# A decoder layer on one core: the second half of an up-projection weight tile is split one work unit later, and the constants are loaded behind the input

## The chip, the cores and the metric

The program runs on one core of a Trainium2 chip. The metric is the device time of one execution in microseconds (us). The runs shown of the kernel before took 1481.33, 1481.35 and 1481.86 us, a median of 1481.35 us.

## The reference, cut to what matters

One layer, 256 tokens, width 2048, everything float32:

```python
def reference(x, p, g_mix, w_in, ..., g_mlp, w_up, w_down, g_ple, w_ple_gate, w_ple_proj):
    h = rmsnorm(x, g_mix)
    proj = h @ w_in                                   # 2048 -> 10240: q, k, v of two mixers, two gates
    qa, ka, va, qb, kb, vb, ga, gb = jnp.split(proj, splits, axis=-1)
    qa = partial_rope(rmsnorm(qa, qn_gain), pos)      # gain and rotation: the constants
    ka = partial_rope(rmsnorm(ka, kn_gain), pos)
    ya = dilated_mixture(qa, ka, va)
    yb = stick_breaking(qb, kb, vb)
    merged = sigmoid(ga) * (ya @ w_branch_a) + sigmoid(gb) * (yb @ w_branch_b)
    x = x + merged @ w_out
    hm = rmsnorm(x, g_mlp)
    x = x + square(relu(hm @ w_up)) @ w_down          # 2048 -> 8192 -> 2048
    hp = rmsnorm(x, g_ple)
    return x + (p @ w_ple_proj) * sigmoid(hp @ w_ple_gate)
```

## The kernel before, in words

Each weight is read from HBM once, in tiles of 1 MB (128 partitions x 8 KB). SP issues these loads (`load`, line 91) into a pool of three buffers called `raw`. A product of two float32 matrices is made of products of their parts: `split` (lines 82 and 83) makes a rounded part `wh` on ACT and the remainder `wl` on DVE, and TensorE (PE) multiplies parts. `split_weights` does this in chunks of 1024 columns; a 1 MB tile gives two chunks. The parts lie in pools of three buffers, `wh` and `wl`. So the next chunk but two can be split only when PE has finished a chunk, and a `raw` buffer is free for the next load when its second chunk has been split.

**The start.** The input stays transposed in `x` (two tiles of 8 rows of 128 features each), the first weights follow in between (`first_weights`, four steps `c`, lines 185 to 204): SP loads a piece of `x`, then the weights that go with it. ACT and DVE make the parts `h` of `x` times gain (lines 85 and 86). The constants (`idt`, an identity for transposes; `cs`, masks and the rotation table; `gq`, the two gains of the norm of q and k) are loaded by POOL's queue at lines 201 to 203. The same queue loads the rows of `x` (`xr`, two tiles of 1 MB, line 229), which lie in the buffers of the two `x` tiles: the first `xr` waits until `x`'s first tile has been read for the last time, the second for the other tile. ACT squares the rows (line 232), and from the sums comes the factor `rt` that scales all results of the first projection; `first_norm` uses it 5 us of the planner's clock behind the first group.

**The MLP.** In stage `s` three streams of work units run interleaved by a table of due times (`together`): the up projection of the next hidden block (`up_units`, 16 units, two per weight tile), a half of the down projection by a fast scheme with seven products (`fast_units`, 7 units, line 545 to 549) and the other half plainly (`plain_units`, 8 units, lines 613 to 615). A generator yields after each unit. An up tile has 16 steps of two matmuls (lines 525 and 526) and yields behind step 7. Results leave PSUM through `add_rows` (line 454, DVE, into `xr`) and through `hidden` (lines 501 to 510). In a fast product, `right` is the sum of a loaded quarter and of `b11`, a further `raw` tile (line 566, DVE).

What stands in which order on an engine is settled when the program is built, by a scheduler that goes by the order of the Python code (its units) and a model of its own. At run time each engine works through its list in order and waits at semaphores.

The lines that the change touches are those of the start and of `up_units`:

```python
            load_rows()
            nc.gpsimd.dma_start(idt, cst[:, C_ID:C_ID + P])
            nc.gpsimd.dma_start(cs, cst)
            nc.gpsimd.dma_start(gq, ...)
...
                parts = split_weights(load(wup[4 * s + g, j], DT, P), DT, P)
                for kt, (wh, wl) in enumerate(parts):
                    ...
                    if kt == 7:
                        yield
```

Of the kernel before, what the change touches and what calls it, by code (L numbers as in the profile page):

```python
# [16 lines left out]
P = 128  # L17
T = 256
D = 2048
DT = D // P  # L20
# [39 lines left out]
def layer_kernel(ctx: ExitStack, tc: tile.TileContext, xt, xm, pt, gains, qkg, cst,  # L60
                 wa, wba, wbb, wo, wup, wdn, wpg, wpp, out):
    nc = tc.nc
# [9 lines left out]
    def block(shape, dtype, name, pool=None):  # L72
        pool = pool or mblk
        return pool.tile(shape, dtype, tag="blk", name=name)

    def bank(tag):
        return psum.tile([P, 512], F32, tag=tag, name=f"ps_{tag}")

    def split(hi, lo, src, scale=None):

        if scale is None:
            nc.scalar.activation(hi, src, AF.Copy)  # L82
            nc.vector.tensor_tensor(lo, src, hi.bitcast(F32), op=ALU.subtract)  # L83
        else:
            nc.scalar.activation(hi, src, AF.Copy, scale=scale)
            nc.vector.scalar_tensor_tensor(lo, src, scale, hi.bitcast(F32),
                                           op0=ALU.mult, op1=ALU.subtract)

    def load(src, nk, cols):
        raw = wts.tile([P, nk, cols], F32, tag="raw", name="raw")  # L90
        nc.sync.dma_start(raw.rearrange("p k c -> p (k c)"), src)
        return raw

    def split_weights(raw, nk, cols, step=None):

        step = step or 1024 // cols
        parts = []
        for k0 in range(0, nk, step):
            n = min(step, nk - k0)
            wh = wts.tile([P, n, cols], F32R, tag="wh", name="wh")  # L100
            wl = wts.tile([P, n, cols], F32R, tag="wl", name="wl")
            split(wh, wl, raw[:, k0:k0 + n, :])
            parts += [(wh[:, i, :], wl[:, i, :]) for i in range(n)]
        return parts
# [11 lines left out]
    def advance(us):  # L116
        clock[0] += us
        while True:
            due = [e for e in pending if e[0] <= clock[0]]
            if not due:  # L120
                return
            e = min(due, key=lambda e: e[:2])
            pending.remove(e)
            e[2](*e[3])

    def flat(a):
        return a.rearrange("p a t -> p (a t)")

    def group_m(chunks, lhs, load=lambda src: weights(src, 4, 512)):

        ps = [bank("mm") for _ in range(2)]
        last, kt = len(lhs) - 1, 0
        for src in chunks:
            for wh, wl in load(src):
                for tt in range(2):
                    t = slice(tt * P, (tt + 1) * P)
                    nc.tensor.matmul(ps[tt], lhs[kt][:, 0, t], wh, start=kt == 0, stop=False)  # L137
                    nc.tensor.matmul(ps[tt], lhs[kt][:, 0, t], wl, start=False, stop=False)  # L138
                    nc.tensor.matmul(ps[tt], lhs[kt][:, 1, t], wh, start=False, stop=kt == last)  # L139
                kt += 1  # L140
                advance(1.3)
        return ps
# [20 lines left out]
    cs = work.tile([P, C_END], F32, tag="cs", name="cs", bufs=1)  # L163
    idt = const.tile([P, P], F32, name="idt")
    gq = const.tile([P, 2, DH], F32, name="gq")
# [6 lines left out]
    def xs(k):  # L172
        return x[k // 8][:, k % 8, :]

    def new_acts(name, n=DT, pool=None):
        tiles = [block([P, 4, 2, T], F32R, f"{name}{i}", pool) for i in range(n // 4)]
        return [tiles[k // 4][:, k % 4, :, :] for k in range(n)]
# [4 lines left out]
    def load_x(a, b):  # L182
        nc.sync.dma_start(x[a // 8][:, a % 8:(b - 1) % 8 + 1, :], xt[:, a:b, :])

    def first_weights(c):

        k = 4 * c
        if c == 0:
            raw = wts.tile([P, 4, 512], F32, tag="raw", name="raw")
            for a, b in ((0, 1), (1, 2), (2, 4)):  # L190
                load_x(a, b)
                nc.sync.dma_start(raw[:, a:b, :].rearrange("p k c -> p (k c)"),
                                  wa[0, 0, :, a * 512:b * 512])
        else:
            load_x(k, k + 4)
            raw = load(wa[0, c], 4, 512)
        for i in range(k, k + 4):
            split(h[i][:, 0, :], h[i][:, 1, :], xs(i), gn[:, 0, i:i + 1])
        if c == 3:
            load_rows()  # L200
            nc.gpsimd.dma_start(idt, cst[:, C_ID:C_ID + P])
            nc.gpsimd.dma_start(cs, cst)
            nc.gpsimd.dma_start(gq, bass.AP(tensor=qkg.tensor, offset=qkg.offset,
                                          ap=[[0, P], [DH, 2], [1, DH]]))
        return split_weights(raw, 4, 512, 1 if c == 0 else 2)
# [19 lines left out]
    def load_rows():  # L225

        xr.extend(block([P, D], F32, f"xr{tt}", blk) for tt in range(2))
        for tt in range(2):
            nc.gpsimd.dma_start(xr[tt], xm[tt])
# [55 lines left out]
    for n, (dst, gain) in enumerate(((qT, gq[:, 0, :]), (kT, gq[:, 1, :]))):  # L285
        for g in range(2):
            if n + g == 0:
                later(5, first_norm, group_m(range(4), h, first_weights))
                continue
            ps = group_m([wa[2 * n + g, c] for c in range(4)], h)  # L290
            for tt in range(2):
                qk_norm(ps[tt], tt, g, gain, dst)
# [89 lines left out]
    for n, dst in enumerate((qS, kS)):  # L382
        for g in range(2):
            later(2, dilated_head, 4 * n + 2 * g)
            later(13, dilated_head, 4 * n + 2 * g + 1)
            ps = group_m([wa[6 + 2 * n + g, c] for c in range(4)], h)
            for tt in range(2):
                raw = work.tile([P, 4, DH], F32, tag="w2", name="sraw", bufs=W2)
# [15 lines left out]
    def cols(g):  # L404
        return slice(g * PIECE, (g + 1) * PIECE)

    for g in range(4):
        later(2, sb_head, 2 * g)
        later(13, sb_head, 2 * g + 1)
        ps = group_m([wa[12 + g, c] for c in range(4)], h)  # L410
        for tt in range(2):
            nc.scalar.activation(ga[tt][:, cols(g)], ps[tt], AF.Copy, scale=rt[:, tt:tt + 1])
    for g in range(4):
        ps = group_m([wba[g, c] for c in range(2)], ya)
        for tt in range(2):
            a = ga[tt][:, cols(g)]
# [17 lines left out]
    for g in range(4):  # L434
        pg = group_m([wa[16 + g, c] for c in range(4)], h)
        sg = []
        for tt in range(2):
            s = work.tile([P, PIECE], F32, tag="w2", name="sg", bufs=W2)
            nc.scalar.activation(s, pg[tt], AF.Sigmoid, scale=rt[:, tt:tt + 1])
            sg.append(s)  # L440
        ps = group_m([wbb[g, c] for c in range(2)], yb)
# [28 lines left out]
    h2 = new_acts("h2_", pool=blk)  # L470
    ss1 = const.tile([P, 2, 4], F32, name="ss1")
    for g in range(4):
        ps = group_m([wo[g, c] for c in range(4)], m)
# [22 lines left out]
    def hidden(s, fast):  # L496

        n = 8 if fast else 4  # L500
        nc.scalar.activation(s, s, AF.Relu)
        r = mw.tile([P, n, P], F32, tag="hr", name="hr", bufs=1)
        nc.scalar.activation(r[:, 0:4, :].rearrange("p a t -> p (a t)"),
                             s.rearrange("p a t -> p (a t)"), AF.Square)
        if fast:
            a21, a11, a22, a12 = (r[:, i, :] for i in range(4))
            nc.vector.tensor_tensor(r[:, 4, :], a11, a21, op=ALU.subtract)
            nc.vector.tensor_tensor(r[:, 5, :], a21, a22, op=ALU.subtract)
            nc.vector.tensor_tensor(r[:, 6, :], r[:, 5, :], a11, op=ALU.subtract)
            nc.vector.tensor_tensor(r[:, 7, :], r[:, 6, :], a12, op=ALU.add)  # L510
        u = hid.tile([P, 2, n, P], F32R, tag="hid", name="u")
        split(u[:, 0], u[:, 1], r)
        return u
# [3 lines left out]
    def up_units(s, out):  # L517

        for g in range(4):
            sums = mw.tile([P, 2, T], F32, tag="hs", name="hs", bufs=2)  # L520
            for j in range(2):
                ps = bank("mm")
                parts = split_weights(load(wup[4 * s + g, j], DT, P), DT, P)
                for kt, (wh, wl) in enumerate(parts):
                    nc.tensor.matmul(ps, wh, flat(h2[kt]), start=kt == 0, stop=False)  # L525
                    nc.tensor.matmul(ps[:, :T], wl, h2[kt][:, 0, :], start=False, stop=kt == DT - 1)  # L526
                    advance(0.347)
                    if kt == 7:
                        yield
                t = mw.tile([P, T], F32, tag="ev", name="ev", bufs=2)  # L530
                nc.scalar.activation(t, ps[:, T:], AF.Copy)
                nc.vector.tensor_tensor(sums[:, j, :], ps[:, :T], t, op=ALU.add)  # L532
                if j == 1:
                    out.append(hidden(sums, (s, 0) in FAST or (s, 1) in FAST))
                yield
# [147 lines left out]
    for _ in up_units(0, hids[0]):  # L683
        pass
# [22 lines left out]
    for g in range(4):  # L707
        ps = [bank("mm") if g % 2 else bank("at") for _ in range(2)]
        for c in range(4):
            for i, (wh, wl) in enumerate(weights(wpg[g, c], 4, PIECE)):  # L710
                kt = 4 * c + i
# [72 lines left out]
```

## Time and profile before

| What | Value |
|---|---|
| Median of the runs | 1481.35 us |
| The profiled execution's own time | 1482.18 us |
| Its span, first to last instruction | 1480.4 us |
| PE (matmul) busy | 1465.0 us, 99% of the span |
| DVE busy | 960.1 us, 65% |
| ACT busy | 822.6 us, 56% |
| POOL busy | 85.5 us, 6% |
| Granted TensorE clock over the span | 0.998 |
| Read from HBM | 297.85 MB, 203 GB/s over the span |

The profiled execution is 0.83 us above the median, and 1.78 us of its time lie outside the span. A matmul counts as busy to its modelled end, and matmuls overlap in the engine, so that a busy PE is not PE at its full rate: where PE loses time is read from the distance of its starts and from its waits.

### The profile page before, as it was taken

What the parts mean: (1) busy time and instruction counts of PE and PEld (TensorE: products, weight loads), DVE (VectorE), ACT (ScalarE), POOL (GpSimd) and SP (SyncE); (2) the same over time, 40 slices, a digit from 0 to 9 for tenths busy, and PEclk for the clock granted to TensorE, in tenths of its full rate; (3) what the DMA queues carried; (4) which work ended last, traced back from release to release, by engine and by line L of the source; (5) the groups of instructions that cost most, each with busy time, mean ns of one, the idle gap of its engine ahead of it and who ended that gap; (6) DMA issues with size and microseconds to landing.
All of it is one profiled execution on the core that took longest, in us unless ns stands there. A gap on an engine that the chain in (4) does not pass through costs nothing.

```text
span 1480.4 us, 17861 instructions
## 1 busy us (share of the span) xinstructions
PE 1465.0 (99%) x6960; PEld 1207.7 (82%) x6960; DVE 960.1 (65%) x1188; ACT 822.6 (56%) x1056; POOL 85.5 (6%) x107
## 2 busy tenths in 40 slices
PE   8999999999999999999999999999999999999998
PEld 6788888888888888888788888888888888888886
DVE  5975555456555555556677768768777777766654
ACT  6544555488834444546655555555555555556553
POOL 0541000000000000000000000000000000000000
PEclk9999999999999999999999999999999999999999
DMA  8555544544455555558677777768777776754562
GB/s 335 193 191 184 171 171 160 181 171 171 170 189 188 193 183 187 199 174 308 200 228 220 234 228 220 235 202 243 224 216 242 217 220 188 232 171 165 206 216 108
DMA packets 46388, 301.10 MB, mean 203 GB/s; under 512 B 5296, under 2 KB 5552, under 8 KB 13152
## 3 DMA queue, kind: packets, MB, share of 16 engines
q1 hardware_dynamic: 39600, 275.01, 53.2%
q0 software_dynamic: 6560, 24.94, 9.1%
q8 instruction: 54, 0.88, 0.2%
q14 instruction: 30, 0.25, 0.0%
q10 hardware_dynamic: 144, 0.02, 0.0%
HBM read 297.85 MB, written 2.10 MB: 203 GB/s over the span
## 4 chain that ended last, share of the span: by engine, by line
PE 94%; DVE 3%; DMA 1%; ACT 1%; issue 1%; SPq 0%; DVEq 0%; ACTq 0%
PE ps_mm L525 16%; PE ps_mm L139 13%; PE ps_mm L138 13%; PE ps_mm L137 13%; PE ps_mm L526 8%; PE ps_mm L615 4%; PE ps_mm L614 4%; PE ps_mm L613 4%; PE ps_at L547 3%; PE ps_at L545 3%; PE ps_at L549 3%; DVE wl L83 1%; PE ps_at L714 1%; PE ps_at L716 1%; PE ps_mm L716 1%; PE ps_mm L714 1%
## 5 line engine op out<-in xcount | busy, mean ns | idle before, releaser
L83 DVE TENSOR_TENSOR wl<-raw,wh 128x1024 fp32r<-128x1024 f32 (+1 forms) x490 | 598.8, 1229 | 396.2 <-ACT wh L82 390.7
L82 ACT ACTIVATE wh<-raw 128x1024 fp32r<-128x1024 f32 (+1 forms) x490 | 515.1, 1054 | 474.5 <-PE ps_mm L139 209.2
L525 PE MATMUL ps_mm<-h,wh 128*128 128x512 f32 x1024 | 365.1, 396 | 0.7 <-ACT wh L82 0.7
L526 PE MATMUL ps_mm<-h,wl 128*128 128x256 f32 x1024 | 287.5, 281 | 2.5 <-DVE wl L83 2.4
L137 PE MATMUL ps_mm<-wh,h 128*128 128x512 f32 x640 | 254.7, 399 | 2.7 <-ACT wh L82 2.7
L138 PE MATMUL ps_mm<-wl,h 128*128 128x512 f32 x640 | 250.4, 391 | 1.8 <-DVE wl L83 1.8
L139 PE MATMUL ps_mm<-wh,h 128*128 128x512 f32 x640 | 250.5, 391 | 0.0
L525 PEld LDWEIGHTS ps_mm<-h,wh 128*128 128x128 f32 x1024 | 192.2, 188 | 45.2 <-ACT wh L82 1.6
L526 PEld LDWEIGHTS ps_mm<-h,wl 128*128 128x128 f32 x1024 | 193.1, 189 | 12.1 <-DVE wl L83 6.9
L137 PEld LDWEIGHTS ps_mm<-wh,h 128*128 128x128 f32 x640 | 120.4, 188 | 28.8 <-ACT wh L82 5.2
L138 PEld LDWEIGHTS ps_mm<-wl,h 128*128 128x128 f32 x640 | 120.7, 189 | 28.3 <-DVE wl L83 4.5
L139 PEld LDWEIGHTS ps_mm<-wh,h 128*128 128x128 f32 x640 | 120.4, 188 | 25.4
L561 POOL DMA_DIRECT2D chain<-in_wdn x42 | 36.3, 864 | 1142.6 <-DVE hs L532 593.8
L615 PE MATMUL ps_mm<-wh,u 128*128 128x512 f32 x256 | 100.2, 391 | 0.0
L614 PE MATMUL ps_mm<-wl,u 128*128 128x512 f32 x256 | 100.2, 391 | 0.0
L613 PE MATMUL ps_mm<-wh,u 128*128 128x512 f32 x256 | 99.9, 391 | 0.0
L83 DVE TENSOR_TENSOR wl<-chain,wh 128x1024 fp32r<-128x1024 f32 x56 | 68.4, 1224 | 29.1 <-ACT wh L82 28.4
L82 ACT ACTIVATE wh<-chain 128x1024 fp32r<-128x1024 f32 x56 | 59.3, 1059 | 48.3 <-PE ps_mm L525 22.6
L547 PE MATMUL ps_at<-wl,u 128*128 128x512 f32 x196 | 80.8, 412 | 0.2 <-DVE wl L83 0.2
L545 PE MATMUL ps_at<-wh,u 128*128 128x512 f32 x196 | 78.9, 402 | 0.0
L549 PE MATMUL ps_at<-wh,u 128*128 128x512 f32 x196 | 77.0, 393 | 0.0
L613 PEld LDWEIGHTS ps_mm<-wh,u 128*128 128x128 f32 x256 | 48.1, 188 | 10.2 <-DVE hs L532 0.3
(198 smaller groups left out, 1737.5 us busy)
## 6 DMA issues: line engine op xcount, KB each, us to landing
raw<-in_wa SPq DMA_DIRECT2D x79, 1024.0 KB, 4.8
raw<-in_wup SPq DMA_DIRECT2D x64, 1024.0 KB, 4.9
raw<-in_wdn SPq DMA_DIRECT2D x50, 1024.0 KB, 4.8
chain<-in_wdn POOLq DMA_DIRECT2D x42, 512.0 KB, 5.8
raw<-in_wo SPq DMA_DIRECT2D x16, 1024.0 KB, 4.8
raw<-in_wpg SPq DMA_DIRECT2D x16, 1024.0 KB, 4.8
raw<-in_wba SPq DMA_DIRECT2D x8, 1024.0 KB, 4.8
raw<-in_wbb SPq DMA_DIRECT2D x8, 1024.0 KB, 4.7
```

The source lines that it names most:

```text
L82: nc.scalar.activation(hi, src, AF.Copy)
L83: nc.vector.tensor_tensor(lo, src, hi.bitcast(F32), op=ALU.subtract)
L137: nc.tensor.matmul(ps[tt], lhs[kt][:, 0, t], wh, start=kt == 0, stop=False)
L138: nc.tensor.matmul(ps[tt], lhs[kt][:, 0, t], wl, start=False, stop=False)
L139: nc.tensor.matmul(ps[tt], lhs[kt][:, 1, t], wh, start=False, stop=kt == last)
L525: nc.tensor.matmul(ps, wh, flat(h2[kt]), start=kt == 0, stop=False)
L526: nc.tensor.matmul(ps[:, :T], wl, h2[kt][:, 0, :], start=False, stop=kt == DT - 1)
L545: nc.tensor.matmul(ps, f[k][:, 0, a, :], wh, start=start and k == 0, stop=False, skip_group_check=not start)
L547: nc.tensor.matmul(ps, f[k][:, 0, a, :], wl, start=False, stop=False, skip_group_check=not start)
L613: nc.tensor.matmul(ps[tt], u[k][:, 0, a, :], wh, start=i + k == 0, stop=False)
L614: nc.tensor.matmul(ps[tt], u[k][:, 0, a, :], wl, start=False, stop=False)
L615: nc.tensor.matmul(ps[tt], u[k][:, 1, a, :], wh, start=False, stop=last)
```

## The change

In step 3 of the start, POOL copies one column of `x`'s second tile into each of the three constants' tiles before it loads them. A load may not overtake the copy, and the copy needs the last piece of `x`: so the three loads start only when `x` has landed. In `up_units` the parts of a tile's second chunk (steps 8 to 15) are made by code behind the `yield`, that is in the second unit of the tile, and not with those of the first chunk.

```diff
@@ first_weights
         if c == 3:
+            for late in (idt, cs, gq.rearrange("p a d -> p (a d)")):
+                nc.gpsimd.tensor_copy(late[:, 0:1], xs(k)[:, 0:1])
             load_rows()
             nc.gpsimd.dma_start(idt, cst[:, C_ID:C_ID + P])
             nc.gpsimd.dma_start(cs, cst)
@@ up_units
-                parts = split_weights(load(wup[4 * s + g, j], DT, P), DT, P)
-                for kt, (wh, wl) in enumerate(parts):
-                    nc.tensor.matmul(ps, wh, flat(h2[kt]), start=kt == 0, stop=False)
-                    nc.tensor.matmul(ps[:, :T], wl, h2[kt][:, 0, :], start=False, stop=kt == DT - 1)
-                    advance(0.347)
-                    if kt == 7:
+                raw = load(wup[4 * s + g, j], DT, P)
+                for k0 in (0, 8):
+                    for i, (wh, wl) in enumerate(split_weights(raw[:, k0:k0 + 8, :], 8, P)):
+                        kt = k0 + i
+                        nc.tensor.matmul(ps, wh, flat(h2[kt]), start=kt == 0, stop=False)
+                        nc.tensor.matmul(ps[:, :T], wl, h2[kt][:, 0, :], start=False,
+                                         stop=kt == DT - 1)
+                        advance(0.347)
+                    if k0 == 0:
                         yield
```

Behind these lines, line numbers grow by 2, and behind `up_units` by 5.

The first place is POOL's list at the start. Before:

```order
L201 DMA idt_84<-in_cst 128x128
L202 DMA cs_83<-in_cst 128x1216
L203 DMA gq_85<-in_qkg 128x256
L229 DMA xr0_247<-in_xm 128x2048
L229 DMA xr1_248<-in_xm 128x2048
```

and now:

```order
L201 COPY idt_84<-x1_74 128x1
L201 COPY cs_83<-x1_74 128x1
L201 COPY gq_85<-x1_74 128x1
L203 DMA idt_84<-in_cst 128x128
L231 DMA xr0_250<-in_xm 128x2048
L231 DMA xr1_251<-in_xm 128x2048
L204 DMA cs_83<-in_cst 128x1216
L205 DMA gq_85<-in_qkg 128x256
```

The loads of `cs` and `gq` moved behind both loads of the rows; the copies and the small load of `idt` stand ahead of the first. On ACT, the two conversions of constants (`tri_r`, `ones_r`) moved from between the first weight splits to behind the first result's scaling (`qraw`).

The second place is DVE in stage 1 of the MLP, around the end of a plain product (`xr0` and `xr1` from `ps_mm`) and of an up tile (`hs`). `raw_6566` and `raw_6569` are the `b11` tile of a fast product in the two kernels, `raw_6592` and `raw_6595` the next up tile. Before:

```order
L566 TENSOR_TENSOR right_6454<-right_6454,raw_6566 128x2048
L532 TENSOR_TENSOR hs_6403<-ps_mm_6404,ev_6473 128x256
L83 TENSOR_TENSOR wl_6502<-raw_6499,wh_6501 128x1024
L83 TENSOR_TENSOR wl_6506<-raw_6499,wh_6505 128x1024
L83 TENSOR_TENSOR wl_6569<-raw_6566,wh_6568 128x1024
L454 SCALAR_TENSOR_TENSOR xr0_247<-ps_mm_6287,r2_5039,xr0_247 128x512
L83 TENSOR_TENSOR wl_6580<-raw_6566,wh_6579 128x1024
L532 TENSOR_TENSOR hs_6403<-ps_mm_6498,ev_6541 128x256
L454 SCALAR_TENSOR_TENSOR xr1_248<-ps_mm_6288,r2_5039,xr1_248 128x512
L83 TENSOR_TENSOR wl_6595<-raw_6592,wh_6594 128x1024
L83 TENSOR_TENSOR wl_6599<-raw_6592,wh_6598 128x1024
```

and now:

```order
L83 TENSOR_TENSOR wl_6505<-raw_6502,wh_6504 128x1024
L537 TENSOR_TENSOR hs_6406<-ps_mm_6407,ev_6476 128x256
L571 TENSOR_TENSOR right_6453<-right_6453,raw_6569 128x2048
L83 TENSOR_TENSOR wl_6525<-raw_6502,wh_6524 128x1024
L83 TENSOR_TENSOR wl_6572<-raw_6569,wh_6571 128x1024
L83 TENSOR_TENSOR wl_6583<-raw_6569,wh_6582 128x1024
L537 TENSOR_TENSOR hs_6406<-ps_mm_6501,ev_6544 128x256
L456 SCALAR_TENSOR_TENSOR xr0_250<-ps_mm_6290,r2_5042,xr0_250 128x512
L456 SCALAR_TENSOR_TENSOR xr1_251<-ps_mm_6291,r2_5042,xr1_251 128x512
L83 TENSOR_TENSOR wl_6598<-raw_6595,wh_6597 128x1024
L456 SCALAR_TENSOR_TENSOR xr1_251<-ps_at_6430,r2_5042,xr1_251 128x512
```

The second split of `b11` moved ahead of `hs` and of both sums, the sum into `right` moved one split further back (between the two splits of one up tile), and the second split of the next up tile moved away from behind its first.

The third place is ACT where stage 1 begins: the splits of an up tile (`raw`) and of the fast product's `chain`. Before:

```order
L82 ACTIVATE wh_6216<-raw_6214 128x1024
L82 ACTIVATE wh_6220<-raw_6214 128x1024
L531 ACTIVATE ev_6187<-ps_mm_6143 128x256
L82 ACTIVATE wh_6245<-chain_6242 128x1024
L501 ACTIVATE hs_6051<-hs_6051 128x512
L503 ACTIVATE hr_6191<-hs_6051 128x512
L82 ACTIVATE wh_6255<-chain_6242 128x1024
```

and now:

```order
L82 ACTIVATE wh_6219<-raw_6217 128x1024
L82 ACTIVATE wh_6244<-chain_6241 128x1024
L536 ACTIVATE ev_6190<-ps_mm_6146 128x256
L82 ACTIVATE wh_6254<-chain_6241 128x1024
L503 ACTIVATE hs_6054<-hs_6054 128x512
L505 ACTIVATE hr_6194<-hs_6054 128x512
L82 ACTIVATE wh_6266<-raw_6217 128x1024
```

The chunks are now split in the order of the units: first half of the up tile, the two of the fast product, second half of the up tile.

## Rows read from the trace of the kernel before

**Rows 1.** The page's head, and where PE waited (line waited for: us, times, longest).

```profile
span 1480.4 us, 17861 instructions
...
PE ps_mm L526 <- DVE wl L83: 2.4, 5, 0.5
...
PE ps_mm L525 <- ACT wh L82: 0.7, 1, 0.7
PE ps_at L547 <- DVE wl L83: 0.2, 1, 0.2
```

**Rows 2.** The chain that ended last, in order of time (start us, us, what).

```profile
24.13 9.70 DMA xr<-in_xm
```

**Rows 3.** Timeline of ACT, then PE, where the second row tile lands.

```profile
33.86 0.63 ACT L232 ACTIVATE junk<-xr 128x512 f32<-128x512 f32 x1 [3.49 <-DMA xr<-in_xm]
...
34.49 1.04 ACT L82 ACTIVATE wh<-raw 128x1024 fp32r<-128x1024 f32 x1
...
36.84 0.50 PE L138 MATMUL ps_mm<-wl,h 128*128 128x512 f32 x1 [0.41 <-DVE wl L83]
```

**Rows 4.** Table by stretch: us, each engine's busy time, clock, DMA share, GB/s.

```profile
4.00:8.00 4.00, 2.84 (x8) 1.05 (x6) 1.05 (x2) 0.79 (x2) 0.00 (x0) 1.00 0.93 289
...
24.00:34.00 10.00, 10.00 (x45) 8.26 (x44) 3.58 (x3) 5.57 (x12) 0.53 (x1) 1.00 0.96 395
```

**Rows 5.** DMA of 4 to 8 us: POOL's queue (q0), packets, MB, share.

```profile
q0 software_dynamic: 186, 0.73, 58.9%
```

**Rows 6.** DMA issues up to 40 us: KB each, median us to landing.

```profile
cs<-in_cst POOLq DMA_DIRECT2D x1, 608.0 KB, 6.3
```

**Rows 7.** Timeline of SP and POOL at the start; then landing times of x's pieces.

```profile
7.83 0.33 SPq L183 DMA_DIRECT2D x<-in_xt  x1
...
1.27 0.71 POOL L201 DMA_DIRECT2D idt<-in_cst  x1 [0.82 <-POOLq L775]
...
14.88 0.53 POOL L229 DMA_DIRECT2D xr<-in_xm  x1 [11.81 <-DMA x<-in_xt]
...
DMA to landing us min/median/max: 2.4/8.0/12.7
```

**Rows 8.** Timeline of DVE, then PE, in stage 1 of the MLP.

```profile
842.65 1.23 DVE L83 TENSOR_TENSOR wl<-raw,wh 128x1024 fp32r<-128x1024 f32 x1
843.80 0.42 DVE L532 TENSOR_TENSOR hs<-ps_mm,ev 128x256 f32<-128x256 f32 x1
844.13 0.74 DVE L454 SCALAR_TENSOR_TENSOR xr<-ps_mm,r,xr 128x512 f32<-128x512 f32 x1
844.79 2.35 DVE L83 TENSOR_TENSOR wl<-raw,wh 128x1024 fp32r<-128x1024 f32 x2
...
844.96 0.39 PE L549 MATMUL ps_at<-wh,u 128*128 128x512 f32 x1
845.19 0.39 PE L525 MATMUL ps_mm<-h,wh 128*128 128x512 f32 x1
846.06 0.39 PE L526 MATMUL ps_mm<-h,wl 128*128 128x256 f32 x1 [0.48 <-DVE wl L83]
```

**Rows 9.** Timeline of ACT just before that.

```profile
841.56 1.06 ACT L82 ACTIVATE wh<-raw 128x1024 fp32r<-128x1024 f32 x1 [1.73 <-PE ps_mm L525]
```

**Rows 10.** Timeline of SP and DVE around the sum into right; then the page's DMA issues.

```profile
825.02 0.33 SPq L91 DMA_DIRECT2D raw<-in_wdn  x1
...
831.93 2.28 DVE L566 TENSOR_TENSOR right<-right,raw 128x2048 f32<-128x2048 f32 x1
...
raw<-in_wdn SPq DMA_DIRECT2D x50, 1024.0 KB, 4.8
```

**Rows 11.** Timeline of DVE in the first norms; then POOL's smallest products by tile.

```profile
41.96 0.69 DVE L251 TENSOR_TENSOR qsq<-qraw 128x512 f32<-128x512 f32 x1
...
47.37 1.78 DVE L251 TENSOR_TENSOR qsq<-qraw 128x512 f32<-128x512 f32 x1
...
L265 POOL TENSOR_TENSOR ro<-qn,cs x32: 311/322/1339, 48.7 to 118.0; 128x64 f32<-128x64 f32 x32
```

## The prediction

> **What bounds the kernel now.** I read the page's head and its list of PE's waits first. PE is busy for 99% of the span, and its waits in the MLP are few: 2.4 us in five waits of L526 for a `wl`, 0.7 us in one of L525 for a `wh`, 0.2 us in one of L547 for a `wl` [rows 1]. So PE bounds nearly everything, and a change of order can give back only what PE loses in such places, and what it loses at the start. In both orders as written out, the mixers between roughly 60 and 670 us are the same.
>
> For the start I read the chain of waits, then the timelines. One transfer stands on the chain there: the second tile of rows, `xr`, 9.70 us from 24.13 [rows 2]. ACT idles 3.49 us for it, squares its rows at 33.86, and only then makes the next weights' `wh` at 34.49; PE, which wants the remainder of these weights, starts late, at 36.84, with 0.41 us of waiting [rows 3]. So PE's stream is tied here to the landing at 33.83 (24.13 + 9.70): whatever earlier work gains is kept only as far as this landing comes earlier too.
>
> What makes it late is the bandwidth: between 24 and 34 us the DMA engines are busy for 0.96 of the time and move 395 GB/s, between 4 and 8 us for 0.93 but at 289 GB/s [rows 4]. In the latter stretch the constants' queue takes 58.9% and moves 0.73 MB [rows 5]. The last piece of `x`, issued at 7.83, needs the longest of all pieces, 12.7 us, and so lands at 20.5; the first `xr` is issued at 14.88 after 11.81 us of POOL's waiting [rows 7].
>
> In the MLP I read DVE and PE side by side in stage 1. PE's L525 starts at 845.19, its L526 not until 846.06, with a listed wait of 0.48 [rows 8]. The `wl` that it wants is the first of two that start at 844.79, and ahead of them stand `hs` (843.80, 0.42), a sum into `xr` (844.13, 0.74) and the `wl` of the `b11` tile's second chunk (842.65, 1.23) [rows 8]. That one waited for its `wh`, which began at 841.56 after 1.73 us of waiting for a buffer that PE still read [rows 9]. The stall is made of order: two small DVE tasks behind a late split.
>
> **The start, step by step.** The constants weigh 64 + 608 + 128 KB = 0.82 MB; `cs` alone is 608 KB and lands 6.3 us behind its issue [rows 6]. Taken out of the stretch from 4 to 8 us, they free 0.82 MB / 395 GB/s = 2.1 us of a fully busy transport, or 0.73 MB / 289 GB/s = 2.5 us at that stretch's own rate [rows 4, 5]. So `x` and the first weights may land 2.1 to 2.5 us earlier, and PE's first products with them.
>
> What PE keeps is set by the second `xr`. For it: the transport has up to 2.1 us less to move. Against it: before its issue now stand, on POOL, a wait for the last piece of `x` (landing at 20.5 before, perhaps 18.4 now), three copies of one column and the issue of `idt`. No row shows such a copy; the nearest is a product of 64 columns, 322 ns [rows 11], so the copies cost 0 to 3 x 0.32 = 1.0 us. The issue costs up to 0.71 [rows 7]. The first `xr` was issued at 14.88; now it cannot be before some 18.4 + 0.7 = 19.1 at least. That is 4 us later, and then both loads of rows run back to back in one queue, with the second no longer issued at 24.13 only when `x`'s second tile has been read. Since the DMA engines were busy throughout, a later start of the first costs nothing while others have work for them, and the second lands when the sum of bytes is through. The bounds are then a second `xr` that lands 2.1 us earlier (all bytes of the constants stand behind it) and one that lands later by a whole transfer, the 9.7 us of [rows 2] behind a first one that ends where it ended. I take half of the possible gain, 1.0 us: the engines have SP's loads to fill the gap that POOL's delay leaves, 0.96 busy as they are [rows 4], which speaks for the good end, but the later start of the first tile must be made up. The two conversions of constants on ACT move behind this point and may stand ahead of a split there, and a statistic on DVE moves behind a `wl`: 0.2 us lost, between 0 and 0.4, the wait of [rows 3]. **Start: -0.8 us**, ends -2.5 - 0.4 (the wait of [rows 3] goes too) = -2.9, and +7.8, worked out under the rivals.
>
> The transfers of `cs` and `gq`, moved behind the rows, would land some 6.3 us behind 34 us, at about 40; their first reader is the norm's product, whose DVE part in the trace follows at 41.96 and 47.37 [rows 11]. I cost that at nothing; the cover is one to seven microseconds.
>
> One row speaks against the copies. The product `qsq` takes 0.69 us at 41.96, and 1.78 us at 47.37 with the same shape [rows 11], where POOL works beside it. The Trainium skill's page "SBUF — State Buffer", section "SBUF: two separate sides", says that VectorE and GpSimd share one pair of ports as an exclusive lock, and that a DVE instruction with two SBUF inputs blocks for the whole of a GpSimd instruction that reads SBUF. By that rule the three copies could hold DVE for up to 1.0 us in the splits ahead of the second `xr`, and the start would give about 0 in place of -0.8. I stay with -0.8: a copy of one column should be nearer to nothing than to the 322 ns of 64 columns [rows 11].
>
> **The MLP, step by step.** No instruction of PE, ACT or DVE is added; the second chunk's `wh` and `wl` move behind the two of the fast product. What goes: L525 to L526 took 846.06 - 845.19 = 0.87 us, and an unhindered step takes 845.19 - 844.96 = 0.23 [rows 8], so one stall costs 0.64, which is 0.16 more than its listed wait. Five of them [rows 1] make 3.2 us. The two others of [rows 1], 0.7 + 0.16 and 0.2 + 0.16, make 1.2. All seven: 4.4 us. In the new order the second split of `b11` stands ahead of `hs` and the sums, and its buffer comes free six matmuls earlier, 6 x 0.23 = 1.4 us. The chain wh, wl, hs, sum moves up by that, more than 0.64, so each stall goes: -4.4, bounds -4.4 and 0.
>
> What comes: the sum into `right` (2.28 us, at 831.93) now stands between the two splits of one up tile, and the load of `b11`, at 825.02 [rows 10], waits for a `raw` buffer that is free only when an up tile's second split is done, now behind two chunks of the fast product, on DVE at least 2 x 1.23 = 2.5 us later [rows 8]. It lands 4.8 us behind its issue [rows 10], so at 832.3 or later: the sum waits, and behind it on DVE the second `wl` of an up tile, at 832.3 + 2.28 + 1.23 = 835.8 or later. That sum had landed data some 2 us ahead before; now nothing is left. No row tells what PE would wait; bounds are 0 and the 0.64 of the stall that goes. The sum comes out almost even by my order of the units, so I take 0.1 for each of the seven: +0.7. **MLP: -3.7 us**, ends -4.4 and about 0.
>
> **Sum.** -0.8 - 3.7 = -4.5 us. The span becomes 1475.9, the execution of the profile 1482.18 - 4.5 = 1477.7; it stood 0.83 above the median of 1481.35, so the forecast is **1476.8 us**.
>
> **The rivals.** *The sum into right takes the place of the stall.* Each of seven places loses 0.64 on the late `b11` tile instead of on the late `wl`. For it: the landing is worked out without a margin. Against it: 1.4 us of room come from the earlier buffer. The MLP then gives 0, the start -0.8: 1480.5 us.
>
> *Slower: the rows land late.* If `x`'s last piece does not land sooner than 20.5 (the change then does not do what it should: other transfers fill the freed time first), the copies and `idt` end at 20.5 + 1.0 + 0.7 = 22.2, the first `xr` needs 9.7 and the second, one queue, another 9.7: 41.6, against 33.83. All of 7.8 us goes to PE, since ACT stands in order behind it: 1481.35 + 7.8 - 3.7 = 1485.4, and slower from the point where the second `xr` lands 3.7 us late, at 37.5. Against it: two transfers in one queue need not follow one another when the engines are otherwise free, and 2 MB at 395 GB/s are 5.3 us, not 19.4.
>
> *The start pays in full.* The transport is through 2.1 us earlier, PE's wait of 0.41 goes, and the conversions cost nothing: -2.5 - 3.7 = -6.2, or 1475.1; with the MLP's whole -4.4 and the start's end of -2.9, 1474.0.
>
> **How the numbers follow.** Some 0.2%, 3 us, is what a measurement of this kernel can tell from no change: bounds 1478.4 and 1484.3. The forecast has 0.54; its own range is 1475.3 to 1478.5 (the start between 0 and -1.6, `right` between 0 and +1.7). The full start has 0.16, the sum into `right` 0.18, late rows 0.12. Faster: 0.50 + 0.16 = 0.66. Same: 0.04 of the forecast's, 0.16 of `right`'s, 0.03 of the late rows = 0.23. Slower: 0.09 of the late rows and 0.02 where `right` waits longer than the old stall = 0.11. The range leaves out the late rows and a little at both ends: 1472.5 (1474.0 less what smaller waits give that no list names) to 1481.5.
>
> **What would show it.** Right: ACT's `junk` of the second `xr` before 33.4; the last piece of `x` in under 12.7 us; no L526 wait of 0.5 at the stages' starts; `hs` and the sums ahead of the late `wl`. Wrong: `right` waiting for a DMA with PE's L525 or L526 waiting behind it; the second `xr` landing behind 34; `qn`'s product on POOL or DVE waiting for `cs`.

## The result: slower by 0.65%, and the profile after

The changed kernel took 1491.21 us in the median of six runs (1489.02 to 1492.67), the kernel before 1481.37 (1481.25 to 1481.86, six runs): a ratio of 1.0065, 95% interval 1.0052 to 1.0078. The forecast was 1476.8 us. The profiled execution took 1490.03 us with a span of 1488.3, 7.9 us more than before.

The page's head and lists of waits, the changed kernel (line waited for: us, times, longest), answer to [rows 1]:

```profile
span 1488.3 us, 17882 instructions
...
PE ps_mm L530 <- DVE wl L83: 10.6, 9, 2.3
...
DVE right L571 <- DMA raw<-in_wdn: 11.5, 7, 2.4
```

L530 is the former L526, L571 the former L566. The five waits of 2.4 us became nine of 10.6 us, and a wait stands there that the kernel before hardly had: the sum into `right` waits for a DMA, once in each of the seven stages.

PE tells where the 7.9 us lie. The MLP is counted here from the first up product behind PE's last eight transposes for `h2`: it starts at 667.94 us instead of 669.04 (1.1 gained at the start). From there to the first transpose of the next norm PE takes 700.28 us instead of 691.31 (9.0 lost); the rest is equal within 0.02 us. So the whole loss is in the MLP.

Timeline of the changed kernel in stage 1: SP, POOL, DVE, then PE. It answers to [rows 8, 10].

```profile
829.73 0.33 SPq L91 DMA_DIRECT2D raw<-in_wdn  x1
...
826.01 0.86 POOL L566 DMA_DIRECT2D chain<-in_wdn  x1 [19.90 <-DVE wl L83]
827.48 0.86 POOL L566 DMA_DIRECT2D chain<-in_wdn  x1 [0.60 <-DVE wl L83]
...
828.48 1.22 DVE L83 TENSOR_TENSOR wl<-raw,wh 128x1024 fp32r<-128x1024 f32 x1
...
837.17 2.29 DVE L571 TENSOR_TENSOR right<-right,raw 128x2048 f32<-128x2048 f32 x1 [1.55 <-DMA raw<-in_wdn]
839.38 2.35 DVE L83 TENSOR_TENSOR wl<-raw,wh 128x1024 fp32r<-128x1024 f32 x2
...
838.95 0.40 PE L619 MATMUL ps_mm<-wl,u 128*128 128x512 f32 x1
840.65 0.39 PE L530 MATMUL ps_mm<-h,wl 128*128 128x256 f32 x1 [1.30 <-DVE wl L83]
```

Read from the top. The `wl` at 828.48 is an up tile's second chunk, now behind both chunks of the fast product. When it ends, at 829.7, a `raw` buffer is free, and SP issues the load of `b11`. By then POOL has issued its two loads that add into `chain`. DVE reaches the sum into `right` at 835.6, waits 1.55 us for `b11`, and the `wl` that PE wants stands behind the sum.

DMA issues of the changed kernel, this load alone (KB each, us to landing), and then the load of `b11` in the kernel before, issued at 825.02, ahead of the two chain loads (826.62 and 828.16):

```profile
raw<-in_wdn SPq DMA_DIRECT2D x1, 1024.0 KB, 7.4
```

```profile
raw<-in_wdn SPq DMA_DIRECT2D x1, 1024.0 KB, 5.0
```

The same megabyte needs 2.4 us more. In the changed kernel it takes from 7.1 to 8.8 us in the seven stages, in the kernel before from 4.9 to 5.4 in six and 7.2 in one.

What each queue moved (q0 is POOL's queue, q1 SP's; packets, MB, share of the engines): the changed kernel from 829 to 833 us, then from 833 to 838; last the kernel before from 827 to 829, with `b11` ahead.

```profile
q0 software_dynamic: 204, 0.77, 105.7%
...
q1 hardware_dynamic: 240, 1.84, 87.3%
q0 software_dynamic: 49, 0.14, 14.8%
...
q1 hardware_dynamic: 98, 0.79, 98.1%
q0 software_dynamic: 1, 0.00, 2.1%
```

So `b11`, issued at 829.73, moves nothing until 833: the engines work for the chain's loads alone. In four of the other six stages SP's queue likewise moves nothing in the 3 us behind the issue of `b11`; in the two others it takes at most 24% of the engines in 4 us. In the kernel before it is the other way round: `b11` moves, and the chain's loads, issued at 826.62 and 828.16, wait.

Table by stretch of the changed kernel (columns as in [rows 4]): first the time in which only the chain's loads move, then that of `b11`, the next up tile and the chain's rest, then around and behind the longest stall of PE.

```profile
829.00:833.00 4.00, 4.00 (x23) 3.43 (x22) 3.95 (x5) 2.65 (x4) 0.00 (x0) 1.00 1.06 193
833.00:838.00 5.00, 5.00 (x26) 4.16 (x25) 3.30 (x4) 2.35 (x3) 0.00 (x0) 1.00 1.02 394
...
744.00:752.00 8.00, 5.74 (x28) 4.56 (x27) 5.21 (x4) 2.12 (x2) 0.00 (x0) 0.90 0.63 214
752.00:760.00 8.00, 7.64 (x33) 5.95 (x32) 4.18 (x6) 4.70 (x7) 0.00 (x0) 0.89 0.42 139
```

While the adding loads run, the DMA engines are as busy as later but move half as much, 193 against 394 GB/s. The last two rows show a second cost. The longest stall lies between two starts of PE at 747.87 and 750.52, 2.4 us more than an unhindered step. Behind it the granted clock is 0.90 and 0.89 of full speed in the mean, that is, at its lower level of 1.2 GHz for part of both stretches. The same stands behind the other long stall, at 1194 us (0.85 and 0.94). The kernel before has 1.00 in every such stretch of the MLP.

### The profile page after: what moved, and what is told of

The parts are those of the page before. It is cut to its first block, busy times and chain, and to the rows that moved or that the text cites. A ratio compares the mean times of both kernels' runs of the same rounds, so it can differ in the third digit from the quotient of the medians.

```text
span 1488.3 us, 17882 instructions
## 1 busy us (share of the span) xinstructions
PE 1467.1 (99%) x6960; PEld 1210.9 (81%) x6960; DVE 963.6 (65%) x1188; ACT 824.3 (55%) x1056; POOL 87.1 (6%) x110
## 4 chain that ended last, share of the span: by engine, by line
PE 87%; DMA 5%; DVE 4%; ACT 2%; issue 1%; SPq 0%; DVEq 0%; ACTq 0%
PE ps_mm L529 13%; PE ps_mm L139 13%; PE ps_mm L138 13%; PE ps_mm L137 13%; PE ps_mm L530 7%; DMA raw<-in_wdn 4%; PE ps_mm L618 3%; PE ps_mm L620 3%; PE ps_mm L619 3%; PE ps_at L552 3%; PE ps_at L550 2%; PE ps_at L554 2%; DVE wl L83 2%; ACT wh L82 1%; PE ps_at L719 1%
## 5 line engine op out<-in xcount | busy, mean ns | idle before, releaser
L530 PE MATMUL ps_mm<-h,wl 128*128 128x256 f32 x1024 | 291.0, 285 | 10.6 <-DVE wl L83 10.6
L530 PEld LDWEIGHTS ps_mm<-h,wl 128*128 128x128 f32 x1024 | 194.5, 190 | 25.5 <-DVE wl L83 22.0
L566 POOL DMA_DIRECT2D chain<-in_wdn x42 | 36.4, 866 | 1151.5 <-DVE wl L83 1151.5
L82 ACT ACTIVATE wh<-chain 128x1024 fp32r<-128x1024 f32 x56 | 59.4, 1061 | 62.0 <-PE ps_mm L529 36.4
L552 PE MATMUL ps_at<-wl,u 128*128 128x512 f32 x196 | 78.3, 399 | 0.4 <-DVE wl L83 0.4
L550 PE MATMUL ps_at<-wh,u 128*128 128x512 f32 x196 | 78.2, 399 | 0.0
```

What stands on the lines that cost most here:

```text
L550: nc.tensor.matmul(ps, f[k][:, 0, a, :], wh, start=start and k == 0, stop=False, skip_group_check=not start)
L552: nc.tensor.matmul(ps, f[k][:, 0, a, :], wl, start=False, stop=False, skip_group_check=not start)
```

## The experiments

The first theory: the loss is `b11`'s load, which inherits a `raw` buffer that the later split holds longer. The rival: parts that are made just in time starve PE in any tile. The constants' part was thought to be a small gain.

**1. The two parts apart, and the one tile apart.** In every stage `b11` takes over the buffer of the first tile of the second group (`g` 1, `j` 0).

```diff
 e1_split: the changed kernel without the copies
-            for late in (idt, cs, gq.rearrange("p a d -> p (a d)")):
-                nc.gpsimd.tensor_copy(late[:, 0:1], xs(k)[:, 0:1])
 e2_const: the kernel before with the copies
 e3_early2: the changed kernel, this one tile split in one piece
+                two = split_weights(raw, DT, P) if (g, j) == (1, 0) else None
 e4_late2: the converse
+                two = split_weights(raw, DT, P) if (g, j) != (1, 0) else None
```

> Only the later split of an up tile's second chunk; constants as before. First theory (the whole loss comes from the later split, and the constants' part is a small gain of 1.1 us at the start): 1481.4 + 9 = about 1491 to 1492 us, with the nine waits of L530 (line numbers shifted by 2) for a wl, 10 us in all. Rival (the two parts of the change disturb each other, or the constants' part costs time later on): clearly below 1490 us.

> Only the constants behind x; up tiles are split as before. First theory: PE reaches the MLP 1.1 us sooner, the MLP has its old waits of seven places, about 3.3 us listed: 1480.3 us. Rival (the constants' part costs or gives nothing by itself): 1481.4 us or more.

> As the changed kernel, but the up tile whose raw buffer the b11 load takes over (group 1, first tile of each stage) is split in one piece as before; the other seven tiles of a stage keep the later split. First theory (the loss is b11's load, which waits for that buffer, lands late and holds the sum into right on DVE, behind which a wl stands): the waits of 1.1 to 2.4 us at L530 are gone, 1477 to 1481 us. Rival (parts that are made just in time starve PE in any tile): 1488 us or more, with L530 waits that move to other tiles.

> The converse: the constants behind x, and only that one tile of each stage (group 1, first tile) has the later split; the other seven are split in one piece. First theory: all of the loss comes back from this tile alone, 1487 to 1492 us, the sum into right waiting for a DMA in each stage. Rival: 1480 to 1482 us, as one tile of eight carries at most an eighth of the loss.

| Kernel | us, median (range) | ratio to before, 95% interval |
|---|---|---|
| before, same chip | 1481.53 (1480.11 to 1482.83) | |
| e1_split | 1490.2 (1487.15 to 1493.04) | 1.0055 (1.0038 to 1.0071) |
| e2_const | 1483.3 (1481.57 to 1484.77) | 1.0015 (1.0006 to 1.0024) |
| e3_early2 | 1482.76 (1480.55 to 1485.57) | 1.0011 (1.0001 to 1.0020) |
| e4_late2 | 1505.92 (1504.3 to 1508.87) | 1.0170 (1.0155 to 1.0185) |

The later split alone makes the loss (e1). Splitting one tile of eight early takes it away (e3), and splitting that tile alone late brings it back, and more (e4): the rival falls. Each time missed its range: e1 by 0.8 us, e3 by 1.8, e4 by 13.9. In e3 and e4 the scheduler also reordered other tasks of PE, ACT and DVE in the MLP, so they show which tile it is and not the price. Waits of e4, the PE's and the sum's (the view of one line: us, times):

```profile
PE ps_mm L530 <- DVE wl L83: 18.8, 7, 3.4
```

```profile
  DMA raw<-in_wdn: 20.5, 7
```

In stage 1 the load of `b11` is issued at 830.27 there and lands 8.5 us later (8.5 to 9.6 in the seven stages). In e3 it lands in 5.1 us and the sum waits for nothing, but five waits of 0.63 us at the old places (844.43 is the first) are back: its MLP takes 691.05 us against 691.31 before. The later split in the seven other tiles is worth next to nothing.

The miss that tells most is e2: the constants' part, a gain of 1.1 us in the profile of the whole change, costs 1.8 us by itself. Timeline of e2_const at the start: POOL, DVE, ACT, PE. It answers to [rows 3, 7].

```profile
18.36 1.24 POOL L201 COPY idt<-x 128x1 f32<-128x1 f32 x1 [17.91 <-DMA x<-in_xt]
19.53 1.20 POOL L201 COPY cs<-x 128x1 f32<-128x1 f32 x1
20.67 0.46 POOL L201 COPY gq<-x 128x1 f32<-128x1 f32 x1
21.07 0.72 POOL L203 DMA_DIRECT2D idt<-in_cst  x1
21.77 0.57 POOL L231 DMA_DIRECT2D xr<-in_xm  x1
...
18.33 2.36 DVE L83 TENSOR_TENSOR wl<-raw,wh 128x1024 fp32r<-128x1024 f32 x2
...
32.06 0.63 ACT L234 ACTIVATE junk<-xr 128x512 f32<-128x512 f32 x1 [7.20 <-DMA xr<-in_xm]
...
36.41 0.63 ACT L234 ACTIVATE junk<-xr 128x512 f32<-128x512 f32 x1 [0.85 <-DMA xr<-in_xm]
...
34.39 0.50 PE L137 MATMUL ps_mm<-wh,h 128*128 128x512 f32 x1 [2.47 <-ACT wh L82]
```

The first load of the rows is issued at 21.77 instead of 14.88, ACT waits 7.20 us for it, and PE starves at 34.39, a place where it did not wait before. This profiled execution is the slowest of its ten; PE reaches the MLP at 672.08, 3.0 us later than before, in e3 and e4, with the same edit at the start, at 669.05 and 669.28. So the start of the change varies between a gain of 1.1 us and a loss of 3.

What differs is again the load that stands ahead. Timeline of the changed kernel at the start, POOL; then what each queue moved from 22 to 24 us, in the changed kernel and in e2:

```profile
18.27 1.23 POOL L201 COPY idt<-x 128x1 f32<-128x1 f32 x1 [17.82 <-DMA x<-in_xt]
19.44 0.18 POOL L201 COPY cs<-x 128x1 f32<-128x1 f32 x1
...
20.53 0.57 POOL L231 DMA_DIRECT2D xr<-in_xm  x1
...
q0 software_dynamic: 79, 0.57, 81.7%
q1 hardware_dynamic: 8, 0.03, 4.0%
...
q1 hardware_dynamic: 91, 0.68, 85.3%
```

In the changed kernel the rows, issued at 20.53, are ahead of SP's weight load of 21.95 and land 5.6 us later. In e2 the copies take longer, SP's load goes out first (20.71), and the rows of 21.77 land 10.3 us later; in e3 and e4 the order is that of e2. All engines have the same lists at the start in these four kernels; why they ran so differently was not tried.

**2. Another buffer for b11, no chain load beside it, and the rows ahead of the copies.** The second `right` buffer is idle while `right` lies in the first.

```diff
 e5_split_own (with the later split), e6_before_own (with the split of before)
-        b11 = load(wdn[s, n, 1, 1], 4, PIECE)
+        b11 = quarter("right", 2, 1, 1)
 e7_split_nochain (with the later split)
-        add_loaded(chain, 1, 1)
 e8_const_xr0 (the split of before)
             load_rows()
+            for late in (idt, cs, gq.rearrange("p a d -> p (a d)")):
+                nc.gpsimd.tensor_copy(late[:, 0:1], xr[0][:, 0:1])
```

> The later split alone (no change to the constants), with b11 loaded into the second right buffer, which is free, in place of a raw buffer. First theory (b11's load waits for the raw buffer that the later split holds longer): no sum into right waits for a DMA, no L528 wait over 1 us, 1476 to 1482 us. Rival (the wait at L528 comes from the later splits themselves): 1487 us or more.

> The kernel before, b11 loaded into the second right buffer. If the five waits of 0.5 us at L526 in the kernel before come from the b11 tile's use of a raw buffer, they go and it takes 1477 to 1479 us; if they come from the splits' order alone, it takes 1481 us as before.

> The later split alone, and the second of the three sums into the chain (two transfers of 512 KB by POOL's queue, a part of the fast scheme's sum) is left out, so that b11's load has the DMA engines for itself. The load took 7.1 to 8.2 us beside these two transfers. If its slowness is needed for the loss, it lands in about 4.8 us and the sum into right waits for 0 us in place of 1.5: 1480 to 1484 us. If the late issue alone makes the loss, the wait stays at 1 us or more: 1488 us or more.

> Up tiles as before; POOL's copies into the constants' tiles read the first row tile in place of x's last piece, so that both loads of the rows are issued ahead of the copies. Theory for the start (the constants' part cost 1.8 us by itself, since the first load of the rows stands behind the wait for x's last piece and three copies of up to 1.2 us and lands late): the first rows land before 25 us, ACT does not wait for them, PE reaches the MLP at 667 to 668 us, 1479 to 1481 us. Rival (the constants themselves land too late or take the bandwidth of the rows there): 1482 us or more, with waits on cs, gq or idt behind 40 us.

| Kernel | us, median (range) | ratio to before, 95% interval | MLP in the profile, us |
|---|---|---|---|
| before, same chip | 1481.65 (1480.73 to 1483.75) | | 691.31 |
| e5_split_own | 1483.62 (1481.02 to 1484.94) | 1.0012 (1.0003 to 1.0021) | 693.26 |
| e6_before_own | 1475.54 (1474.65 to 1477.21) | 0.9959 (0.9945 to 0.9973) | 685.14 |
| e7_split_nochain | 1477.16 (1475.38 to 1478.65) | 0.9966 (0.9953 to 0.9979) | 685.83 |
| e8_const_xr0 | 1480.69 (1479.81 to 1481.78) | 0.9993 (0.9984 to 1.0003) | 691.72 |

e7 is the clearest. It leaves out the second of the three sums into the chain, two loads in each stage, which the layer needs; PE, ACT, DVE and SP have the same lists in the MLP as in e1 and in the change, entry by entry. With these loads gone, `b11`, issued at 825.88 just as late behind the later split, lands in 4.9 us, the sum into `right` no longer waits, and of the waits at L528 (the old L526) hardly anything is left. All PE's waits of e7:

```profile
PE ps_at L161 <- DVE warm L159: 1.5, 1, 1.5
PE ps_mm L137 <- ACT wh L82: 1.4, 2, 1.0
PE ps_mm L528 <- DVE wl L83: 0.8, 2, 0.4
PE ps_mm L138 <- DVE wl L83: 0.5, 1, 0.5
```

So the later split as such does what was forecast, and more: 691.31 - 685.83 = 5.5 us less in the MLP. Part of this may be the 14 transfers that e7 leaves out; the seven stalls that were named are gone, and e7 took 2.8 us less than its range. The late issue alone costs nothing; late and behind the chain's loads costs 700.28 - 685.83 = 14.5 us. Step by step along PE's list, 10.9 of these are lost at the seven places where the `wl` stands behind the sum, some 3 just behind the two longest of them, at the lower clock, and little is left for another cause.

e5 went half as expected and lies between its two ranges: no sum waits for a DMA and one wait of 0.4 us is left at L528, but PE now waits in the fast product. Its PE waits, and then the load that feeds the worst of them (issued at 1156.75, with two chain loads, issued from 1154.45 on, ahead of it):

```profile
PE ps_at L550 <- DVE wl L83: 4.2, 6, 0.8
PE ps_at L548 <- ACT wh L82: 2.9, 3, 1.4
```

```profile
raw<-in_wdn SPq DMA_DIRECT2D x1, 1024.0 KB, 10.7
```

It is the same collision at another load. With the splits of before (e6) a load still falls behind the chain's two (in stage 1 at 830.84, 6.8 us), but PE waits for none of them, and six of the seven old stalls go: 1.5 us better than its range. In e5 and e6 the scheduler also set other orders on PE, ACT, DVE and SP, so this gain is that of the buffer together with the order that came with it.

In e8 the copies read the first row tile, and both loads of the rows stand ahead of them. Timeline of e8_const_xr0, POOL and ACT:

```profile
13.59 0.70 POOL L231 DMA_DIRECT2D xr<-in_xm  x1 [13.15 <-DMA x<-in_xt]
22.84 0.54 POOL L231 DMA_DIRECT2D xr<-in_xm  x1 [8.54 <-DVE h L86]
23.37 0.20 POOL L202 COPY idt<-xr 128x1 f32<-128x1 f32 x1
...
31.81 0.63 ACT L234 ACTIVATE junk<-xr 128x512 f32<-128x512 f32 x1 [2.76 <-DMA xr<-in_xm]
```

The second tile lands 2.0 us sooner than in [rows 3], ACT does not wait for the first tile, and PE reaches the MLP at 666.98, 2.1 us sooner. The median's gain, 1.0 us, is at the edge of what could be told (the interval reaches 1.0003), but between e2, 1.8 us over its kernel before, and e8, 1.0 us under, the order of the copies and loads is worth 2.7 us.

**3. The two gains together, and b11 ahead of the chain's loads.**

```diff
 e9_best: the kernel before with the edits of e6 and e8
 e10_split_hoist: the later split, b11's load one unit earlier
         right = quarter("right", 2, 0, 1)
+        b11 = load(wdn[s, n, 1, 1], 4, PIECE)
         yield
-        b11 = load(wdn[s, n, 1, 1], 4, PIECE)
```

> The kernel before, with b11 in the second right buffer and with the constants' copies reading the first row tile (both loads of the rows ahead of the constants). If the two gains lie in different places and add up: 1475.5 less 1.0 = 1474 to 1475 us, no L525 or L526 wait over 0.4 us in the MLP but the one at 732 us, PE at the MLP by 667 to 668 us. If one of them needs the other's absence: 1475.5 us or more.

> The later split alone, with b11's load one unit earlier in the program, so that it takes another raw buffer, that of a tile split in one go or earlier, and stands ahead of the two transfers into the chain. Theory (the loss hangs on which load inherits the late buffer and on its place before or behind the chain's transfers): b11 lands in about 5 us, the sum into right waits for no DMA, and at most the up tile that now inherits the late buffer waits: 1476 to 1483 us. Rival (any load behind a later split is late by as much): 1487 us or more, with the wait at another tile.

e9 took 1474.22 us (1472.56 to 1475.03), a ratio of 0.9952 (0.9939 to 0.9966) to 1480.94: 6.7 us faster than the kernel before, as expected from the two gains. All PE's waits of e9:

```profile
PE ps_mm L137 <- ACT wh L82: 2.1, 2, 1.1
PE ps_at L161 <- DVE warm L159: 1.5, 1, 1.5
PE ps_mm L138 <- DVE wl L83: 0.8, 2, 0.5
PE ps_mm L527 <- ACT wh L82: 0.7, 1, 0.7
```

e10 took 1528.97 us, 1.0326 (1.0312 to 1.0340): the rival's side, by far. Timeline of e10_split_hoist, stage 1: SP, DVE, POOL, ACT.

```profile
825.56 1.84 SPq L91 DMA_DIRECT2D raw<-in_wdn  x2
837.23 3.62 SPq L91 DMA_DIRECT2D raw<-in_wup  x2
...
830.46 2.29 DVE L569 TENSOR_TENSOR right<-right,raw 128x2048 f32<-128x2048 f32 x1 [1.09 <-DMA raw<-in_wdn]
...
834.75 1.76 POOL L564 DMA_DIRECT2D chain<-in_wdn  x2 [22.15 <-DVE wl L83]
...
845.81 2.00 ACT L82 ACTIVATE wh<-raw 128x1024 fp32r<-128x1024 f32 x2 [5.31 <-DMA raw<-in_wup]
```

`b11` now lands 4.9 us behind its issue at 825.56, as the theory had it, though the sum into `right` still waits for it, 8.2 us in seven stages: the scheduler put the sum earlier, ahead of the chain's splits, and the chain's loads ten of PE's matmuls later. An up tile now inherits the late buffer: issued at 837.23, behind the chain's loads of 834.75, it lands 8.6 us later, and all work waits for it. PE's waits in L527 are eight, 28.9 us. That a load behind the chain's loads lands late holds here too; the theory's estimate of the price, "at most the up tile", was far too small. How much of it is the scheduler's other order was not tried apart.

## Why the prediction was wrong

- **What goes in the MLP (-4.4): right for the waits.** In e7 and e6 the waits at the stages' starts are gone, and the MLP is 5.5 and 6.2 us shorter. Of this some 3.5 are waits (e6 keeps one of 0.7, e7 has two new ones of 0.4). Another 2.0 to 2.5 us stand in steps too short for the list, which the sum did not have: those from L547 to L549 took 47.4 us in all, 45.4 in e6 and 44.9 in e7 (there L550 to L552). "The stall is made of order" left out the buffer: in e6 six of the seven stalls go with every split in its old unit, by another buffer for `b11` and the list order that came with it.
- **What comes (+0.7): the step that failed.** It said the sum into `right` "comes out almost even", with `b11` landing "4.8 us behind its issue", the median of [rows 10]. The late issue was well sized: at least 2.5 us, and 2.7 in e7 (825.88 - 825.02 = 0.9 by the clock, 1.5 by which its MLP starts sooner, and 0.3 less lost by then). But in [rows 10] that load stood ahead of the chain's two loads, and 2.5 us later it stands behind them: 7.1 to 8.8 us instead of 5.0. Seven waits of the sum, 11.5 us in all, reached PE. The loss against e7 is 14.5 us, twenty times the term. The POOL queue's loads were never placed in the sum; each term looked at its own queue.
- **The rival "the sum into right takes the place of the stall" named the place and the wait**, but bounded the price by the stall that goes (0.64 each). No row bounds a wait for a DMA by that. Taken as there, from PE's starts, its stalls were 1.1 to 2.4 us, and the two longest also cost clock.
- **The start (-0.8): its cause was right, its size is not stable.** `x` and the first weights came sooner: `x`'s last piece was issued at 6.35 instead of 7.83, and the copy that waits for it starts at 18.27, so it landed some 2 us sooner than 20.5, as forecast. In the profile of the change the second `xr` landed at 32.25 and 1.1 us were left; in e2, with the same edit, 1.8 us were lost in the median. What failed is "a later start of the first costs nothing while others have work for them": in e2 SP's load went first, the rows moved nothing from 22 to 24 us, and the second `xr` landed at 36.4. That the profile of the change came near -0.8 is luck, since there the rows happened to go out first. The rival "the rows land late" has the right mechanism, the first load of the rows behind the copies, with a price of 3.0 us in the slowest profile instead of 7.8.
- **The copies (0 to 1.0 us): wrong by their neighbour.** Two of them took 1.24 and 1.20 us in e2, as long as DVE's `wl` beside them, and 0.20 in e8 when DVE was idle. The Trainium skill's page "SBUF — State Buffer", section "SBUF: two separate sides", was used in one direction only: by it the pair of ports goes to whichever starts first. The traces agree with the rule in this direction too: in e2 DVE's splits kept their 1.2 us, and POOL's copies took as long. The bound of 1.0 us drawn from 322 ns was too low: 2.9 us for three in e2, 1.6 in the change.

## What to carry to other kernels

When a change makes a buffer come free later, ask which load inherits it, and what is then ahead of that load on the DMA engines, other queues included: a load's time from a table holds only for the place in the traffic that it had. A wait in an engine's list costs what stands behind it, so a DMA-fed task that nobody needs soon (here the sum into `right`) should not stand ahead of one that PE needs next; this last was argued and not tried by itself. Ahead of reordering the splits, look for an idle buffer: one line that moved `b11` to another pool gave 6 us, with every split still in its old unit, though the scheduler's order changed with it.

## What the runs showed of the hardware

Two loads that add into SBUF, 512 KB each, kept the DMA engines busy at half the rate: 193 GB/s at a share of 1.06, against 394 GB/s at 1.02 for mostly plain loads just behind. A 1 MB load that another queue issued behind them moved nothing for some 3 us, until they were nearly through. Behind PE's two longest stalls of the changed kernel (listed with 2.3 and 2.1 us, at 748 and 1195) the granted clock fell to its lower level, 1.2 GHz, for part of the next microseconds; the five of 1.0 to 1.3 us left it at 1.00. In e4 it fell behind five of seven stalls of 2.3 to 3.4 us and stayed at 1.00 behind two of 2.6, so the length of the stall alone does not tell. e7 and e6, without such stalls, show 1.00 throughout the MLP. Whether the wider spread of the changed kernel (3.7 us, against 0.6 of the kernel before on the same chip) comes from that was not tried.
